# A hybrid decoder layer on one core: fillers kept back behind forgetting-attention stacks, fillers of stick-breaking heads shared out by scan length, and stacks filled by one copy and one subtraction

## The chip, the cores and the metric

The kernel runs on one core of one Trainium2 chip. The metric is device microseconds from the start of the program to its end. Before the change three runs took 2321.92, 2323.00 and 2324.88 us, the median being 2323.0 us.

## What is computed

One decoder layer for 1024 positions of width 1024, in float32. A half step of a SwiGLU network (`x + 0.5 * swiglu(norm(x))`, inner width 2816), then two attentions side by side on the same normed input, a second half SwiGLU step, and a gated embedding. The attentions have eight heads of 64 each:

```
forgetting:      logit[t,s] = q_t.k_s/8 + sum_{s<j<=t} log f_j,  causal softmax, times v
                 (q and k are rms-normed per head, with gains)
stick-breaking:  beta[t,s] = sigmoid(q_t.k_s/8)
                 A[t,s] = beta[t,s] * prod_{s<j<t} (1 - beta[t,j])   for s < t, times v
merged = sigmoid(g_fox) * (y_fox @ w_branch_fox) + sigmoid(g_sb) * (y_sb @ w_branch_sb)
x = x + merged @ w_out
```

Products are made to nearly full float32 precision out of a high part (rounded to the fast matmul type) and a low part (what the rounding lost): high x high + high x low + low x high.

## The kernel before

The program runs stage by stage: first feed-forward step, attention, output projection, second feed-forward step, embedding. The change touches the attention stage, `attention()`, which takes the 16 heads one after the other, 0 to 7 forgetting, 8 to 15 stick-breaking.

**A head.** It has four steps, c = 0 to 3, each with two blocks of 128 queries, i = 2c and 2c + 1. `scores` makes for both blocks the products with all keys up to the block (n = 128(i + 1) columns). It needs the head's *stacks*: Q (128 x 1024, upper 64 partitions the high part of q, lower 64 the low part), KH (the high part of k, twice, on both halves) and KL (the low part of k, twice). The products are the matmuls of lines 1040 (with KH) and 1041 (with KL). Then a forgetting head adds the forget sums and takes row maxima on DVE (line 1045), the exponential on ACT (line 1051), a reciprocal on DVE (line 1052) and the scaling on POOL (line 1053). A stick-breaking head takes two sigmoids on ACT (lines 1048, 1049) and then products along the row by scans on DVE (line 1016), whose time grows with n, and multiplies on POOL (lines 1063 and 1067).

`apply` handles the step before (`prev`), so the scores of step c come between the scores and the values of step c - 1; at c = 0 it is step 3 of the head before. For each pair of key blocks it transposes the probabilities on PE (line 1092, into one of two "pt" banks of PSUM), copies the high part on ACT (line 1094), subtracts on DVE for the low part (line 1095), and multiplies with the values on PE (line 1114). The scans of the step's second block are held in `later` and issued between those subtractions.

**Filling.** Between these pieces the function `take` (called `fill` inside `scores` and `apply`) issues other matmuls, a few at a time: projections for later heads (line 799: v, and q and k of forgetting heads; line 807: q and k of stick-breaking heads, and the gates), and the *forgetting stacks* (line 901: four transposes of normed q and k). These are generators that yield their cost in microseconds after each matmul (0.109 or 0.216). In each head `take` is called 22 times: 7 times at c = 0 (2 in `scores`, 5 in `apply` for the previous head's c = 3), then 4, 5 and 6 times. Each call raises the allowance by total/22, total being the cost of the head's fillers, and issues until the count reaches it; at the head's end `take(True)` drains what is left. PE runs strictly in the order so written (the helper `pe`); the other engines' order comes from the framework's scheduler.

Filling units write to one of two "pf" banks of PSUM. A unit of line 799 or 807 is followed by a copy and mostly a subtraction that empty the bank (lines 105 and 106 for v, 929 for a gate, 965 for the embedding), a stack unit by `fill_stacks`.

**Stacks.** `fill_stacks` gets 512 columns with q on partitions 0 to 63 and k on 64 to 127 in one bank. It makes two copies on ACT (lines 886, 887 with gain for forgetting heads; 881, 882 without for stick-breaking ones), two subtractions on DVE (888, 889 or 883, 884), and two DMAs on the SP queue (890, 891) which bring k's parts to the upper half of KH and KL. Each head needs two such halves; they are made while the head before runs. Stack buffers are two deep. The order in which fillers stand is given by the list `fill`: with forgetting heads a stack half stands between projections, or two halves meet at a head's border (the last of one list and the first of the next, at the starts of heads 2, 4 and 6).

Of the kernel before, what the change touches and what calls it, by code (L numbers as in the profile page):

```python
# [13 lines left out]
AF = mybir.ActivationFunctionType  # L14
ALU = mybir.AluOpType
# [21 lines left out]
def tile_hybrid_decoder_layer(  # L37
# [6 lines left out]
    nc = tc.nc  # L44
# [11 lines left out]
    def slot(tag, shape, dt=F32):  # L56
        pad = -shape[-1] % 16
        t = sb.tile([*shape[:-1], shape[-1] + pad], dt, tag=tag, bufs=BUFS[tag], name=nm(tag))
        return t[:, :, :shape[-1]] if pad else t
# [6 lines left out]
    def bank(tag):  # L66
        return pp.tile([P, 512], F32, tag=tag, bufs=PSUM[tag], name=nm("ps"))

    def ps1():
        ring[0] += 1  # L70
        return bank(("pt", "pf", "pt", "pf")[ring[0] % 4])
# [8 lines left out]
    def pe(ins):  # L80
        order("pe", ins)
# [7 lines left out]
    def f(ap):  # L89
        return ap.bitcast(F32)  # L90
# [783 lines left out]
    def new_stacks():  # L874
        return slot("Q", [P, S], F32R), slot("KH", [P, S], F32R), slot("KL", [P, S], F32R)

    def fill_stacks(stacks, ps, cs, gain=None):
        Q, KH, KL = stacks
        a, b = slice(0, HD), slice(HD, P)
        if gain is None:  # L880
            nc.scalar.copy(Q[a, cs], ps[a, :])
            nc.scalar.copy(KH[b, cs], ps[b, :])
            nc.vector.tensor_sub(Q[b, cs], ps[a, :], f(Q[a, cs]))
            nc.vector.tensor_sub(KL[b, cs], ps[b, :], f(KH[b, cs]))
        else:
            nc.scalar.activation(Q[a, cs], ps[a, :], AF.Copy, scale=gain[a, :])
            nc.scalar.activation(KH[b, cs], ps[b, :], AF.Copy, scale=gain[b, :])
            nc.vector.scalar_tensor_tensor(Q[b, cs], ps[a, :], gain[a, :], f(Q[a, cs]), ALU.mult, ALU.subtract)
            nc.vector.scalar_tensor_tensor(KL[b, cs], ps[b, :], gain[b, :], f(KH[b, cs]), ALU.mult, ALU.subtract)  # L889
        nc.sync.dma_start(f(KH[a, cs]), f(KH[b, cs]))  # L890
        nc.sync.dma_start(f(KL[a, cs]), f(KL[b, cs]))

    def fox_stack_units(cell, hh, out_cell, new_bank=fill_bank):
        def unit(half):
            if half == 0:
                out_cell["st"] = new_stacks()
            cs = slice(half * 512, half * 512 + 512)
            N = cell["n"][half]
            ps = new_bank()
            for q in range(4):  # L900
                pe(nc.tensor.transpose(ps[:, q * P:(q + 1) * P], N[:, q, hh].rearrange("p s d -> p (s d)"), identf[:]))
                yield 0.109
            fill_stacks(out_cell["st"], ps, cs, gqk)
        return [(0.436, unit(0)), (0.436, unit(1))]

    def sb_stack_units(head, out_cell):
        c0 = head * HD

        add_load(out_cell, lambda: wload([kp(win)[:, :, SQ + c0:SQ + c0 + HD], kp(win)[:, :, SK + c0:SK + c0 + HD]], KD, P))

        def unit(half):
            weights(out_cell)
            if half == 0:
                out_cell["st"] = new_stacks()
            ps = bank("pf")
            yield from feat_steps(ps, half, out_cell["w"])
            fill_stacks(out_cell["st"], ps, slice(half * 512, half * 512 + 512))
        return [(24 * 0.216, unit(0)), (24 * 0.216, unit(1))]
# [303 lines left out]
    def attention():  # L1222
# [5 lines left out]
        def fst(h, *to):  # L1228
            return fox_stack_units(qk[h // 2], h % 2, stacks[h], *to)
# [38 lines left out]
        f = [fst(h) for h in range(1, 8)]  # L1268
# [19 lines left out]
        def load_fb(h):  # L1288
            if h < 8:
                head = fox_pairs[h // 2] * 2 + h % 2  # L1290
                fbs[h]["t"] = slot("GF", [P, S])
                nc.sync.dma_start(fbs[h]["t"][:], fd[head].partition_broadcast(P))
# [3 lines left out]
        for h in range(16):  # L1296
            fox = h < 8
            if h % 2 == 0:
                idx = fox_pairs[h // 2] if fox else 4 + (h - 8) // 2
                ys[h // 2] = {"t": slot("Y", [P, S]), "idx": idx}  # L1300
            head = ys[h // 2]["idx"] % 4 * 2 + h % 2
            v = (vf1, vf0, vs0, vs1)[h // 4]
            load_fb(h + 1)
            total = sum(u[0] for u in fill[h])
            state = [0.0, 0.0]
            gens = [u[1] for u in fill[h]]

            def take(last=False):
                state[0] += total / 22
                while gens and (last or state[1] < state[0]):  # L1310
                    cost = next(gens[0], None)
                    if cost is None:
                        gens.pop(0)
                    else:
                        state[1] += cost
            for c in range(4):
                y0, y1 = Y_AT.get((h, c), ((), ()))
                split_y(*y0)
                load_y(*y1)
                step = {"fox": fox, "c": c, "head": head, "st": stacks[h], "v": v, "y": ys[h // 2], "last": h == 15}  # L1320
                if fox:
                    step["fb"] = fbs[h]
                later = []
                scores(step, take, later if prev is not None else None)
                if prev is not None:
                    apply(prev, take, later)
                prev = step
            take(True)
        rest = seq(*[g for _, g in fox_branch[7:]])
        apply(prev, lambda: run(islice(rest, 6)))  # L1330
        run(rest)
        yt = ys[7]["t"]
        for half in range(2):
            cs = slice(half * 512, half * 512 + 512)
# [8 lines left out]
    def load_y(*ks):  # L1343
        for k in ks:
            if k == 0:
                Y_["t"] = slot("X", [P, 4, S])
            nc.sync.dma_start(Y_["t"][:, k % 4, :], yd[k])

    def split_y(*ks):
        for k in ks:  # L1350
            g, i = divmod(k, 4)
            if i == 0:
                yT.append((slot("H", [P, 4, S], F32R), slot("H", [P, 4, S], F32R)))
            hi, lo = yT[g]
            split(hi[:, i, :], lo[:, i, :], Y_["t"][:, i, :], nc.scalar, nc.vector, True)
# [84 lines left out]
    nc.vector.tensor_scalar(gqk[0:HD, :], gqk[0:HD, :], HD ** -0.5, None, ALU.mult)  # L1440

    attention()

    od = dp.tile([4, P, 7, 512], F32, name="branch_sums")
    xm = dp.tile([S, D], F32, name="x_mix")
    for m in range(5, KD):
        w = wload([kp(w_branch_fox[0])[:, :, m * P:(m + 1) * P]], 4, P)
        A.append(slot(("RN", "Q", "KH")[m - 5], [P, S]))
        for half in range(2):
            ps = bank(("sc", "sc", "sc", "pf", "pt", "pf")[2 * (m - 5) + half])  # L1450
# [11 lines left out]
    for m in range(KD):  # L1462
# [13 lines left out]
        for half in range(2):  # L1476
            ps = ps1()
# [161 lines left out]
```

## Time and profile before

| what | us |
|---|---|
| median of three runs | 2323.0 |
| the profiled execution | 2324.2 |
| its span (first to last instruction) | 2322.3 |
| first score matmul of head 0 to that of head 8 | 851.3 to 1144.7 |
| from there to the last value matmul of head 15 | 1144.7 to 1442.7 |

The profiled execution is 1.2 us above the median, and 1.9 us of its time lie outside the span. A row of a group reads: line, engine, operation, tile written <- tiles read, shapes, count | busy us, mean ns of one | idle time of the engine just before them, and what ended it. A row of waits reads: engine, tile and line that waited <- what it waited for: us in total, times, longest. A row of a window reads: stretch, its length, busy time and instructions of PE, PEld (weight loads, beside PE), DVE, ACT and POOL, then the granted TensorE clock, the DMA engines' share and GB/s.

### The profile page before, as it was taken

How to read it: one execution, taken by the hardware profiler on the slowest of the kernel's cores; microseconds unless marked ns; L12 is line 12 of the kernel's file. 1: busy time of each engine (PE TensorE's matmuls, PEld its weight loads, DVE VectorE, ACT ScalarE, POOL GpSimd, SP SyncE). 2: the span in 40 equal slices, each digit the busy share in tenths (PEclk: the TensorE clock that was granted, in tenths of full speed). 3: DMA queues.
4: the chain of work that ended last, by engine and by line, in shares of the span. 5: the costliest groups of instructions: out<-in, count | busy, mean ns of one | idle time of the engine just before them, and what ended most of it. 6: DMA issues, size and time to landing. Idle time of an engine off the chain costs nothing.

```text
span 2322.3 us, 30570 instructions
## 1 busy us (share of the span) xinstructions
PE 2255.0 (97%) x11402; PEld 1909.7 (82%) x11402; DVE 1526.4 (66%) x2296; ACT 1018.1 (44%) x1819; POOL 811.4 (35%) x747
## 2 busy tenths in 40 slices
PE   8999999999999999988998989999999999999999
PEld 6888888888888988988787777888888888888887
DVE  8755555778786336556578787688755555778752
ACT  7333333333454455565655564246333333333431
POOL 2444444200002345645466665500444444200111
PEclk9999999999999999999999999999999999999999
DMA  3333232655233341222202335642333232655232
GB/s 136 108 106 106 98 119 87 228 216 203 92 109 128 110 127 52 60 64 60 64 19 64 87 96 190 220 180 82 106 107 105 100 117 87 227 217 203 74 104 88
DMA packets 179782, 275.48 MB, mean 119 GB/s; under 512 B 26921, under 2 KB 103081, under 8 KB 179634
## 3 DMA queue, kind: packets, MB, share of 16 engines
q1 hardware_dynamic: 179632, 273.53, 35.1%
q8 instruction: 90, 1.47, 0.3%
q14 instruction: 58, 0.48, 0.1%
q10 hardware_dynamic: 2, 0.00, 0.0%
HBM read 189.83 MB, written 75.27 MB: 114 GB/s over the span
## 4 chain that ended last, share of the span: by engine, by line
PE 85%; DVE 8%; ACT 4%; issue 2%; POOL 1%; DMA 0%; SPq 0%; ACTq 0%; DVEq 0%; POOLq 0%
PE ps L556 38%; PE ps L454 21%; PE ps L799 7%; PE ps L1556 4%; DVE RN L1016 3%; PE ps L1361 3%; PE ps L1114 2%; PE ps L807 2%; PE ps L506 2%; PE ps L1092 2%; DVE PT L1095 1%; PE ps L959 1%; PE ps L228 1%; PE ps L1040 1%; PE ps L1041 1%
## 5 line engine op out<-in xcount | busy, mean ns | idle before, releaser
L454 PE MATMUL ps<-H,H 128*128 128x512 f32 x2184 | 497.8, 389 | 1.2 <-DVE X L462 1.2
L454 PEld LDWEIGHTS ps<-H,H 128*128 128x128 f32 x2184 | 409.3, 188 | 86.8 <-issue 2.0
L556 PE MATMUL ps<-H,WL 128*128 128x512 f32 x1116 | 265.0, 389 | 0.8 <-ACT WL L105 0.8
L556 PEld LDWEIGHTS ps<-H,WL 128*128 128x128 f32 x1116 | 209.4, 188 | 44.7 <-ACT WL L105 1.2
L556 PE MATMUL ps<-H,Q 128*128 128x512 f32 x612 | 146.0, 389 | 0.0
L462 DVE SCALAR_TENSOR_TENSOR X<-ps,X 128x512 f32<-128x512 f32 x168 | 108.9, 683 | 51.0 <-PE ps L454 51.0
L1095 DVE TENSOR_TENSOR PT<-ps,PT 128x512 fp32r<-128x512 f32 (+1 forms) x160 | 99.9, 629 | 61.9 <-ACT PT L1094 60.9
L556 PEld LDWEIGHTS ps<-H,Q 128*128 128x128 f32 x612 | 114.9, 188 | 23.9
L799 PE MATMUL ps<-WH,H 128*128 128x256 f32 x768 | 121.7, 296 | 12.2 <-DVE KL L889 7.1
L1114 PE MATMUL ps<-PT,X 128*128 128x256 f32 (+1 forms) x640 | 106.8, 288 | 27.3 <-DVE PT L1095 24.7
L556 PE MATMUL ps<-X,WL 128*128 128x512 f32 x552 | 132.6, 389 | 0.0
L1114 PEld LDWEIGHTS ps<-PT,X 128*128 128x128 f32 x640 | 91.0, 190 | 42.2 <-DVE PT L1095 34.1
L139 POOL TENSOR_TENSOR WL<-RAW,WH 128x512 fp32r<-128x512 f32 (+1 forms) x84 | 99.0, 1201 | 74.6 <-ACT WH L129 42.1
L556 PEld LDWEIGHTS ps<-X,WL 128*128 128x128 f32 x552 | 103.6, 188 | 21.5
L799 PEld LDWEIGHTS ps<-WH,H 128*128 128x128 f32 x768 | 105.5, 197 | 15.3 <-issue 7.7
L1094 ACT CAST PT<-ps 128x512 fp32r<-128x512 f32 (+1 forms) x160 | 87.0, 551 | 65.6 <-PE ps L1092 62.9
L807 PE MATMUL ps<-H,WH 128*128 128x512 f32 x384 | 111.6, 404 | 1.6 <-ACT PT L929 1.6
L219 POOL TENSOR_SCALAR ss<-ss 128x1 f32<-128x1 f32 x28 | 8.5, 304 | 296.9 <-ACT WL L215 231.9
L556 PE MATMUL ps<-H,PT 128*128 128x512 f32 x456 | 108.8, 389 | 0.0
L1053 POOL TENSOR_TENSOR T<-T,l 128x128 f32<-128x128 f32 (+3 forms) x64 | 73.1, 1147 | 98.7 <-DVE l L1052 94.1
L1016 DVE TENSOR_TENSOR_SCAN RN<-GF,RN 128x127 f32<-128x127 f32 (+2 forms) x96 | 102.8, 1071 | 2.6
L1092 PE MATMUL ps<-identf,T 128*128 128x128 f32 x576 | 92.6, 278 | 10.6 <-DVE PT L1095 7.7
(438 smaller groups left out, 4887.2 us busy)
## 6 DMA issues: line engine op xcount, KB each, us to landing
hidden<-PT SPq DMA_DIRECT2D x40, 512.0 KB, 3.1
WH<-in_ffn_w_gate_dram SPq DMA_DIRECT2D x38, 512.0 KB, 5.5
Q<-hidden SPq DMA_DIRECT2D x24, 512.0 KB, 6.8
hidden<-RN SPq DMA_DIRECT2D x22, 512.0 KB, 2.6
KH<-in_ffn_w_up_dram SPq DMA_DIRECT2D x20, 512.0 KB, 6.3
KL<-in_ffn_w_up_dram SPq DMA_DIRECT2D x20, 512.0 KB, 6.9
T<-in_ffn_w_down_dram SPq DMA_DIRECT2D x20, 512.0 KB, 4.4
X<-in_x_dram SPq DMA_DIRECT2D x16, 512.0 KB, 9.5
```

The lines of the kernel that those rows point to most:

```text
L139: ins = eng_lo.tensor_sub(lo[part], raw[part], f(hi[part]))
L454: pe(nc.tensor.matmul(groups[g][t][:], act[:, a, k, t * P:(t + 1) * P], wt[:, b, k, :], start=(fresh and n == 0), stop=(i in (6, 1, 4) and ...
L462: nc.vector.scalar_tensor_tensor(xs, groups[g][t][:], scale, xs, ALU.mult, ALU.add)
L556: pe(nc.tensor.matmul(ps[:], hl[:, a, k, :], rhs(m, b, k), start=(first and i == 0), stop=(final and i == 11), skip_group_check=True))
L799: pe(nc.tensor.matmul(ps[:, :n], hT[t // 4](a, k)[:, (t % 4) * P:(t % 4 + 1) * P], w[k // 4][b][:, k % 4, :n], start=(i == 0), stop=(i == ...
L807: pe(nc.tensor.matmul(ps[:], w[a][:, k, :], hT[half](b, k), start=(i == 0), stop=(i == 23)))
L1016: order("dve", nc.vector.tensor_tensor_scan(*args))
L1092: pe(nc.tensor.transpose(ps[:, col:col + P], step["pr"][j][:, kb * P:(kb + 1) * P], identf[:]))
L1094: high = nc.scalar.copy(pt[:, 0, :width], ps[:, :width])
L1095: low = nc.vector.tensor_sub(pt[:, 1, :width], ps[:, :width], f(pt[:, 0, :width]))
L1114: pe(nc.tensor.matmul(o, lh, r, start=(kpair == c and i == 0), stop=(kpair == 0 and i == 3)))
L1556: pe(nc.tensor.matmul(ps, hT[t // 4](a, k)[:, (t % 4) * P:(t % 4 + 1) * P], pl["w"][d, k // 2][b][:, k % 2, cs], start=(i == 0), stop=(i = ...
```

## The change

Three edits.

1. `fill_stacks` copies all 128 partitions at once to KH, and subtracts all 128 at once into KL. KH[0:64] then holds q's high part and KL[0:64] q's low part; two new DMAs on SP bring them to Q, and then the two old ones overwrite KH[0:64] and KL[0:64] with k's parts. So four DMAs a half instead of two, and the last two may only be issued once the first two have read.
2. `fox_stack_units` yields 1.5 more after `fill_stacks` (`pause`) and counts it in the unit's cost: `take` issues no filling until the allowance has caught up. Where a unit is drained (`run_all` ahead of head 0, `take(True)` at a head's end) the pause has no effect.
3. In stick-breaking heads the filling is no longer spread evenly over the 22 calls, but 14%, 19%, 29% and 38% of it go to c = 0, 1, 2 and 3 (before: 32%, 18%, 23% and 27%). In forgetting heads it stays even.

```diff
         if gain is None:
-            nc.scalar.copy(Q[a, cs], ps[a, :])
-            nc.scalar.copy(KH[b, cs], ps[b, :])
-            nc.vector.tensor_sub(Q[b, cs], ps[a, :], f(Q[a, cs]))
-            nc.vector.tensor_sub(KL[b, cs], ps[b, :], f(KH[b, cs]))
+            nc.scalar.copy(KH[:, cs], ps[:])
+            nc.vector.tensor_sub(KL[:, cs], ps[:], f(KH[:, cs]))
         else:
-            nc.scalar.activation(Q[a, cs], ps[a, :], AF.Copy, scale=gain[a, :])
-            nc.scalar.activation(KH[b, cs], ps[b, :], AF.Copy, scale=gain[b, :])
-            nc.vector.scalar_tensor_tensor(Q[b, cs], ps[a, :], gain[a, :], f(Q[a, cs]), ALU.mult, ALU.subtract)
-            nc.vector.scalar_tensor_tensor(KL[b, cs], ps[b, :], gain[b, :], f(KH[b, cs]), ALU.mult, ALU.subtract)
-        nc.sync.dma_start(f(KH[a, cs]), f(KH[b, cs]))
-        nc.sync.dma_start(f(KL[a, cs]), f(KL[b, cs]))
-
-    def fox_stack_units(cell, hh, out_cell, new_bank=fill_bank):
+            nc.scalar.activation(KH[:, cs], ps[:], AF.Copy, scale=gain[:])
+            nc.vector.scalar_tensor_tensor(KL[:, cs], ps[:], gain[:], f(KH[:, cs]), ALU.mult, ALU.subtract)
+        for dst, src in ((Q[a, cs], KH[a, cs]), (Q[b, cs], KL[a, cs]), (KH[a, cs], KH[b, cs]), (KL[a, cs], KL[b, cs])):
+            nc.sync.dma_start(f(dst), f(src))
+
+    def fox_stack_units(cell, hh, out_cell, new_bank=fill_bank, pause=1.5):
         def unit(half):
...
             fill_stacks(out_cell["st"], ps, cs, gqk)
-        return [(0.436, unit(0)), (0.436, unit(1))]
+            yield pause
+        return [(0.436 + pause, unit(0)), (0.436 + pause, unit(1))]
...
-            state = [0.0, 0.0]
+            state = [0.0, 0.0, 0]
+            share = (7 / 22, 4 / 22, 5 / 22, 6 / 22) if fox else (0.14, 0.19, 0.29, 0.38)
...
             def take(last=False):
-                state[0] += total / 22
+                state[0] += total * share[state[2]] / (7, 4, 5, 6)[state[2]]
...
+                state[2] = c
                 scores(step, take, later if prev is not None else None)
```

What moves on PE at the border of heads 3 and 4, where two stack halves follow each other. Before (line 901 are stack transposes, 1114 values of head 3, 1040 and 1041 scores of head 4, 799 and 807 filling, 1092 probability transposes):

```order
L807 MATMUL ps_8290<-H_4868,WL_7712 128x512 x3
L901 MATMUL ps_8366<-identf,RN_7716 128x128 x4
L1114 MATMUL ps_8313<-PT_8344,X_5815 128x256 x4
L1040 MATMUL ps_8390<-KH_8277,Q_8276 128x128
L1041 MATMUL ps_8390<-KL_8278,Q_8276 128x128
L901 MATMUL ps_8400<-identf,RN_7715 128x128 x4
L799 MATMUL ps_8429<-WH_8178,H_4504 128x256 x3
L1040 MATMUL ps_8437<-KH_8277,Q_8276 128x256
L1041 MATMUL ps_8437<-KL_8278,Q_8276 128x256
L799 MATMUL ps_8429<-WH_8178,H_4504 128x256
```

After, at the same place (lines stand three to four numbers lower: 897 for 901, 1111 for 1114, 1037 and 1038 for 1040 and 1041, 1089 for 1092):

```order
L807 MATMUL ps_8290<-H_4868,WL_7720 128x512 x2
L897 MATMUL ps_8358<-identf,RN_7724 128x128 x4
L1111 MATMUL ps_8317<-PT_8322,X_5815 128x256
L1111 MATMUL ps_8317<-PT_8322,X_5815 128x128 x2
L1111 MATMUL ps_8317<-PT_8322,X_5815 128x256
L1111 MATMUL ps_8317<-PT_8336,X_5815 128x256 x4
L1111 MATMUL ps_8317<-PT_8350,X_5815 128x256 x4
L1037 MATMUL ps_8390<-KH_8251,Q_8250 128x128
L1038 MATMUL ps_8390<-KL_8252,Q_8250 128x128
L897 MATMUL ps_8400<-identf,RN_7723 128x128 x4
L1037 MATMUL ps_8415<-KH_8251,Q_8250 128x256
L1038 MATMUL ps_8415<-KL_8252,Q_8250 128x256
```

The first stack half now stands ahead of all twelve value matmuls, and behind the second one the scores and then the probability transposes (line 1089) follow with no line 799 between.

On PE at c = 0 of head 12, a stick-breaking head; before:

```order
L1040 MATMUL ps_11619<-KH_11273,Q_11272 128x128
L1041 MATMUL ps_11619<-KL_11274,Q_11272 128x128
L807 MATMUL ps_11627<-H_4869,WH_11267 128x512 x4
L1040 MATMUL ps_11635<-KH_11273,Q_11272 128x256
L1041 MATMUL ps_11635<-KL_11274,Q_11272 128x256
L807 MATMUL ps_11627<-H_4868,WH_11267 128x512 x3
L1092 MATMUL ps_11645<-identf,T_11517 128x128
L1092 MATMUL ps_11645<-identf,T_11539 128x128 x2
```

and after:

```order
L1037 MATMUL ps_11619<-KH_11273,Q_11272 128x128
L1038 MATMUL ps_11619<-KL_11274,Q_11272 128x128
L807 MATMUL ps_11627<-H_4869,WH_11267 128x512 x2
L1037 MATMUL ps_11633<-KH_11273,Q_11272 128x256
L1038 MATMUL ps_11633<-KL_11274,Q_11272 128x256
L807 MATMUL ps_11627<-H_4869,WH_11267 128x512
L1089 MATMUL ps_11641<-identf,T_11494 128x128
L1089 MATMUL ps_11641<-identf,T_11533 128x128 x2
```

One or two filling matmuls stand at each call for three or four; over the head's four steps they are 11, 13, 21 and 27 now and were 24, 13, 17 and 20.

On SP, the stack of head 12 (KH_11273, KL_11274, Q_11272) and its neighbours (line 119 loads weights); after:

```order
L887 DMA Q_11272<-KH_11273 64x512
L887 DMA Q_11272<-KL_11274 64x512
L887 DMA KH_11273<-KH_11273 64x512
L887 DMA KL_11274<-KL_11274 64x512
L119 DMA RAW_12240<-in_w_in_dram 128x8x64
L887 DMA Q_11272<-KH_11273 64x512
L887 DMA Q_11272<-KL_11274 64x512
L119 DMA RAW_12240<-in_w_in_dram 128x8x64
L887 DMA KH_11273<-KH_11273 64x512
L887 DMA KL_11274<-KL_11274 64x512
```

There were one KH and one KL row for each half before; a weight load stood between the two of the second half, as one now stands between its two pairs.

## Prediction

> **What bounds the kernel now.** I read the page first, then busy time over the two attention stages, then who TensorE waited for in each, then the instructions around the longest waits. The page's head:
>
> ```profile
> span 2322.3 us, 30570 instructions
> PE 2255.0 (97%) x11402; PEld 1909.7 (82%) x11402; DVE 1526.4 (66%) x2296; ACT 1018.1 (44%) x1819; POOL 811.4 (35%) x747
> ```
>
> PE is busy 97% of the span, so only PE's idle time and its slow clock can be won, and the change touches only the attention. Busy time there, forgetting heads in the first row, stick-breaking heads in the second (length; PE, PEld, DVE, ACT, POOL busy; granted clock; DMA):
>
> ```profile
> 851.30:1144.70 293.40, 267.65 (x1930) 250.24 (x1929) 173.00 (x550) 168.80 (x356) 159.21 (x163) 0.98 0.22 60
> 1144.70:1442.70 298.00, 270.29 (x1572) 231.02 (x1571) 238.75 (x332) 174.37 (x376) 179.71 (x200) 0.98 0.30 87
> ```
>
> PE is idle 25.7 us in the first and 27.7 us in the second, 53 us in all: no more than that, and the slow clock, is in reach. PE's waits, the forgetting stage's six rows ahead, the stick-breaking stage's behind "..." (us in total, times, longest):
>
> ```profile
> PE ps L799 <- DVE KL L889: 7.1, 3, 2.8
> PE ps L799 <- DVE X L106: 4.5, 4, 1.8
> PE ps L807 <- ACT PT L929: 1.6, 1, 1.6
> PE ps L901 <- ACT PT L929: 0.9, 1, 0.9
> PE ps L799 <- ACT PT L965: 0.6, 1, 0.6
> ...
> PE ps L1114 <- DVE PT L1095: 23.2, 24, 1.8
> ```
>
> The five rows of the forgetting stage add up to 14.7 us; all but 0.4 us (one wait at L106) is the first matmul of a filling unit behind a stack's four transposes (L901), or such transposes themselves: 14.3 us. The unit before held one of the two "pf" banks, the stack takes the other for 0.4 us, and then the next unit asks for a bank that nobody has emptied yet. The longest kind, at the start of head 2:
>
> ```profile
> 916.18 0.68 ACT L886 ACTIVATE Q<-ps,gqk 64x512 fp32r<-64x512 f32 x1
> 916.63 0.66 PE L901 MATMUL ps<-identf,RN 128*128 128x128 f32 x4
> 916.87 0.68 ACT L887 ACTIVATE KH<-ps,gqk 64x512 fp32r<-64x512 f32 x1
> 917.59 0.74 DVE L888 SCALAR_TENSOR_TENSOR Q<-ps,gqk,Q 64x512 fp32r<-64x512 f32 x1 [0.36 <-ACT KH L887]
> 918.35 0.76 DVE L889 SCALAR_TENSOR_TENSOR KL<-ps,gqk,KH 64x512 fp32r<-64x512 f32 x1
> 919.25 0.71 PE L799 MATMUL ps<-WH,H 128*128 128x256 f32 x4 [1.97 <-DVE KL L889]
> ```
>
> Two stacks in a row fill both banks; four instructions of some 0.7 us empty the first. Such waits also cost clock. Pairs of rows, a stretch of 3.4 us and the stretch that follows it:
>
> ```profile
> 916.75:920.16 3.41, 1.44 (x12) 1.23 (x12) 2.76 (x7) 2.91 (x7) 0.43 (x2) 1.00 0.17 38
> 920.20:923.60 3.40, 3.40 (x19) 3.40 (x18) 2.24 (x7) 0.99 (x3) 0.03 (x1) 0.50 0.50 116
> 998.70:1002.10 3.40, 0.84 (x7) 0.46 (x5) 1.22 (x4) 3.31 (x6) 1.74 (x2) 1.00 0.14 12
> 1002.10:1008.90 6.80, 5.64 (x27) 5.67 (x27) 4.03 (x11) 3.70 (x8) 1.01 (x2) 0.50 0.66 188
> 1073.80:1077.20 3.40, 1.57 (x13) 1.60 (x14) 2.93 (x5) 1.99 (x5) 0.40 (x1) 1.00 0.23 53
> 1077.20:1080.60 3.40, 3.40 (x18) 3.40 (x17) 1.61 (x7) 1.31 (x4) 0.61 (x1) 0.50 0.44 101
> 1166.00:1169.30 3.30, 1.50 (x10) 1.27 (x9) 3.27 (x4) 0.58 (x2) 3.30 (x3) 1.00 0.00 0
> 1169.40:1172.70 3.30, 3.30 (x14) 2.91 (x13) 3.18 (x6) 2.44 (x6) 2.16 (x4) 0.50 0.99 225
> 1387.80:1391.20 3.40, 1.50 (x8) 1.03 (x7) 3.40 (x4) 1.85 (x3) 1.31 (x2) 1.00 0.93 337
> 1391.20:1398.00 6.80, 6.21 (x20) 5.24 (x21) 6.18 (x7) 2.33 (x8) 5.55 (x6) 0.50 0.45 146
> ```
>
> Each time PE was busy 0.84 to 1.57 us of 3.4, the granted clock in the next stretch was 0.50. The three in the forgetting stage follow the bank waits at the starts of heads 2, 4 and 6; they last 3.4, 6.8 and 3.4 us, and half speed costs half of 13.6: 6.8 us. The two in the other stage last 10.1 us and cost 5.1.
>
> In the stick-breaking stage the waits come in a fixed place. Head 12, its four steps c = 0 to 3:
>
> ```profile
> 1288.50:1297.80 9.30, 9.30 (x60) 8.15 (x59) 4.18 (x8) 4.66 (x10) 2.05 (x5) 1.00 0.07 26
> 1297.80:1302.80 5.00, 4.89 (x27) 4.04 (x26) 4.18 (x5) 3.23 (x7) 4.01 (x4) 1.00 0.76 222
> 1302.80:1310.60 7.80, 7.10 (x41) 5.99 (x41) 7.62 (x12) 5.45 (x13) 7.05 (x9) 1.00 0.82 276
> 1310.60:1322.50 11.90, 9.52 (x53) 7.55 (x52) 11.61 (x14) 7.76 (x15) 7.69 (x8) 1.00 0.06 14
> ```
>
> At c = 0 PE has no gap and DVE is idle more than half; at c = 3 DVE is busy 11.61 of 11.90 us (long scans) and PE idle 2.4 us. That imbalance is what shares by scan length act on.
>
> **The change part by part.** What a stack half's instructions cost (busy us, mean ns, idle before):
>
> ```profile
> L887 ACT ACTIVATE KH<-ps,gqk 64x512 fp32r<-64x512 f32 x16 | 10.9, 682 | 0.3
> L881 ACT CAST Q<-ps 64x512 fp32r<-64x512 f32 x16 | 9.3, 584 | 14.2 <-PE ps L807 14.2
> L889 DVE SCALAR_TENSOR_TENSOR KL<-ps,gqk,KH 64x512 fp32r<-64x512 f32 x16 | 12.1, 757 | 0.4
> L884 DVE TENSOR_TENSOR KL<-ps,KH 64x512 fp32r<-64x512 f32 x16 | 11.1, 695 | 0.4
> L1094 ACT CAST PT<-ps 128x512 fp32r<-128x512 f32 (+1 forms) x160 | 87.0, 551 | 65.6 <-PE ps L1092 62.9 <-ACT T L1051 1.1 <-ACT RN L864 0.6
> L1095 DVE TENSOR_TENSOR PT<-ps,PT 128x512 fp32r<-128x512 f32 (+1 forms) x160 | 99.9, 629 | 61.9 <-ACT PT L1094 60.9 <-DMA RAW<-in_w_in_dram 0.2
> ```
>
> *One copy, one subtraction.* The trace has no 128-partition form of these, but L1094 and L1095 do the like on 128 partitions in 551 and 629 ns (some with 384 columns): no dearer than on 64. So 16 + 16 copies go from ACT (10.9 + 9.3 = 20 us) and as many subtractions from DVE (12.1 + 11.1 = 23 us). Nearly all of it lies beside busy PE; it counts only as a bank that comes free some 1.4 us earlier, and as 0.69 us less DVE at c = 3, both inside the next two terms.
>
> *The two added DMAs a half.* They take the copies' place in Q, and the two old ones now have to wait for the new ones to have read KH and KL. The like of them:
>
> ```profile
> KH<-KH SPq DMA_DIRECT2D x30, 128.0 KB, 2.2
> ```
>
> A stack half is thus ready about two landings behind its subtraction, 4.4 us, not one. I cost it at nothing: columns 512 to 1023 are first read at c = 2, some 12 us later, and the first half of most stacks is ready one step or more ahead. Between nothing and 3 us each for heads 10, 11 and 15 is the bound (rival c).
>
> *Pauses.* Behind fourteen stack halves (those of heads 1 to 7) filling now stays away for 1.5 us of its count. In the new order one or two of the attention's own groups stand between a stack's transposes and the next filling matmul (before, the filling followed at once), so the bank has been emptied by then and the 14.3 us go. What is late next: the attention's own chain, bare of filling there. From transposes to a probability tile's low part there is 0.27 + 0.55 + 0.63 us and two handovers, about 1.6 us, or 2.5 with one stack copy and one subtraction in the queue ahead. Counting in the new order the PE work between the last transposes and the matmuls that need them at the eleven places (at head 5, c = 1, only two stack transposes), the shortfall is 2.5 us against 1.6 and 9.4 against 2.5. The first transposes of the next head may wait for its softmax: 0 to 3.6. Together 2.5 to 13; I take 9, since these queues do hold stack work there. Half clock: two of the three stretches go with their cause, 5.1 of 6.8 us (bounds 0 and 6.8). Forgetting stage: -14.3 + 9 - 5.1 = **-10.4**.
>
> *Shares.* By the order, head 12 gets at c = 0, 1, 2, 3 now 11, 13, 21, 27 filling matmuls for 24, 13, 17, 20 (two fewer here, drained elsewhere). One costs 0.216 us by the count in the kernel; the chain of waits has, for seven in a row,
>
> ```profile
> 1157.27 1.62 PE ps L807 x7
> ```
>
> that is 0.23 each. At c = 0 2.8 us of PE work goes, leaving 6.5. There four rounds of transposes, copy and subtraction over two "pt" banks are serial in pairs; that chain from the step's start I make 7.0 to 8.5 us; I take 7.7: -1.6. At c = 2 0.9 us comes and 0.7 was idle, but not all usable: +0.4. At c = 3 1.5 us comes into 2.4 idle, while DVE loses 0.69 of a step it fills: 0. That is -1.2 a head, eight heads -9.6; bounds -2.6 (c = 0 without a gap) and +1.9 (c = 0 as long as before, and the added work on top of the old waits). One of the two half-clock stretches, that at 1166 in a step that gets more filling, goes: -1.7 (0 to -5.1). Stage: **-11.3**.
>
> Sum: 2324.2 - 10.4 - 11.3 = 2302.5 for the profiled execution. That one was 1.2 us above the median of the runs, so 2301.3: **2301 us**.
>
> *The clock rule.* The rows above give half clock after 3.4 us with PE busy 25 to 46%. [...]
>
> **The rivals.**
> (a) Slower: filling is cover, and where it is taken away the copy-and-subtract chain stands bare. Fourteen pauses then cost the 13 us bound, the half clock stays, and c = 0 stays 9.3 us while c = 2 and 3 grow: -1.3 + 8 x 1.9 = +14, 2337. It decides from +0.7 us a head on, where it eats the 5.3 us that the pauses bring at my price. For it: DVE at 97% of c = 3. Against: DVE is 45% busy at c = 0.
> (b) Shares bring nothing, since DVE sets the head: only the -10.4 stays, 2312.6.
> (c) Stacks come late. DMA queue issues wait behind weight loads:
>
> ```profile
> SPq L119 <- ACT WH L129: 113.7, 18, 25.0
> ```
>
> One such load stood 25 us. If one stands between a stack's DMAs, or landing takes 4 to 5 us, heads 10, 11 and 15 start 1 to 5 us late: about +8, 2309.
> (d) The pauses don't do what they say: the drain at a head's end ignores them, so bank waits stay; then only -11.3, 2312.
> [...]
> (f) Better: new waits 2.5, all half clock of the first stage gone, -2.0 a head: -18.6 - 16 - 1.7 = -36, 2287.
>
> **How the numbers follow.** Forecast 0.42 (own range 2294 to 2308), (a) 0.10, (b) 0.15, (c) 0.08, (d) 0.07, (e) 0.05, (f) 0.13. A range of 2286 to 2318 takes in all but (a) and the far ends of (b) and (f). A measurement tells about 0.2% (4.6 us) from no change. Faster by more 0.81: all but (a), and a part of (b), (c) and (d); within 0.09; slower 0.10.
>
> **What would show it.** In PE's waits the rows of L799 and L807 on the stack's subtraction, L106 and L929 should nearly vanish, and rows of L1114 and L1092 on DVE's L1095 grow in the forgetting stage by 5 to 13 us. Granted clock at the starts of heads 2, 4 and 6 should be 1.00. Head 12 should last 32 to 33 us, c = 0 near 7.7 with small gaps, c = 3 still near 12 with under 1.5 idle. DVE's busy time in the two stages should fall by 23 us and ACT's by 20. A wait of L1040 or L1041 on a DMA of a stack at heads 10, 11 or 15 would be (c). I am wrong if c = 0 stays above 9, or c = 3 grows.

## The result and the profile after

The changed kernel takes **2287.4 us** (median of 4 runs, 2287.38 to 2287.47) against 2323.9 of the kernel before (2321.92 to 2326.29): a ratio of 0.984, 95% interval 0.9825 to 0.986, so 36.5 us less. The forecast was 2301, with a range of 2286 to 2318. The sign was right and the time lies within the range, at its lower end, where rival (f) stood. The gain is 1.7 times the one forecast.

The page's head after the change:

```profile
span 2285.6 us, 30594 instructions
PE 2242.3 (98%) x11402; PEld 1900.6 (83%) x11402; DVE 1498.9 (66%) x2264; ACT 999.5 (44%) x1787; POOL 805.7 (35%) x747
```

Span less PE's busy time is PE's idle time: 67.3 us before, 43.3 now. PE's busy time fell as well, by 12.7 us, with the same 11402 matmuls. Before, the granted clock stood at half for 23.9 us (five stretches), and matmuls took longer there: those of L799 on WH 415 ns between 920.2 and 923.6 us (median of 12) for a median of 283 over the whole trace. Now no stretch of half clock is left between the start and the last microseconds of the program (from 2283.4 us on). DVE lost 27.5 us and ACT 18.6.

The two attention stages, in the columns of before (length; PE, PEld, DVE, ACT, POOL busy; granted clock; DMA):

```profile
851.90:1123.53 271.63, 259.82 (x1931) 244.51 (x1930) 158.84 (x535) 157.73 (x341) 159.41 (x163) 1.00 0.30 82
1123.53:1406.20 282.67, 265.04 (x1572) 227.19 (x1571) 227.89 (x317) 167.71 (x360) 171.74 (x200) 1.00 0.38 105
```

The forgetting stage is 21.8 us shorter (forecast 10.4), the other 15.3 (forecast 11.3). PE's idle time in them is 11.8 us for 25.7, and 17.6 for 27.7. PE's waits after, the forgetting stage ahead of "...", the stick-breaking stage behind:

```profile
PE ps L1089 <- DVE PT L1092: 3.4, 4, 1.1
PE ps L1111 <- DVE PT L1092: 2.8, 5, 1.3
PE ps L1111 <- ACT PT L1091: 2.6, 3, 1.5
PE ps L1089 <- POOL T L1050: 1.3, 1, 1.3
PE ps L799 <- ACT PT L962: 0.3, 1, 0.3
PE ps L799 <- DVE KL L885: 0.2, 1, 0.2
...
PE ps L1111 <- DVE PT L1092: 9.0, 13, 1.0
PE ps L1089 <- DVE PT L1092: 6.5, 7, 1.8
```

The bank waits behind stacks (lines 799, 807 and 897) came to 14.7 us and are 0.7 with a wait of 0.2 at line 897. What is left are waits of the attention's own chain: 10.1 us in the first stage. Those were there before too, and this is the comparison that the prediction did not make: its list of that stage's waits has the five rows of the banks and leaves these four out. The same rows of before, same stage:

```profile
PE ps L1092 <- DVE PT L1095: 5.3, 6, 1.4
PE ps L1114 <- DVE PT L1095: 1.6, 2, 1.2
PE ps L1114 <- ACT PT L1094: 1.5, 1, 1.5
PE ps L1092 <- POOL T L1053: 1.2, 2, 0.8
```

They add up to 9.6. So chain waits grew by 0.5 us, net, under the three edits together, where 9 were forecast.

The start of head 2 after the change, PE alone, the place of the 1.97 us wait that the prediction shows:

```profile
914.81 0.62 PE L897 MATMUL ps<-identf,RN 128*128 128x128 f32 x4
...
915.51 0.28 PE L799 MATMUL ps<-WH,H 128*128 128x256 f32 x1
915.62 0.49 PE L1089 MATMUL ps<-identf,T 128*128 128x128 f32 x3
915.87 1.32 PE L799 MATMUL ps<-WH,H 128*128 128x256 f32 x9
917.03 0.60 PE L1089 MATMUL ps<-identf,T 128*128 128x128 f32 x4
```

None of these rows has a wait in brackets: the scores follow the stack's transposes (L897), then filling (L799) and probability transposes (L1089) alternate. Head 12's steps c = 0, 2 and 3, whose rows of before the prediction has:

```profile
1259.57:1266.46 6.89, 6.82 (x48) 5.95 (x47) 4.18 (x8) 3.61 (x9) 2.15 (x5) 1.00 0.10 38
...
1271.60:1280.57 8.97, 8.30 (x45) 6.76 (x45) 8.79 (x12) 4.39 (x11) 8.38 (x9) 1.00 0.71 222
1280.57:1292.52 11.95, 11.09 (x60) 9.08 (x59) 10.92 (x13) 7.75 (x15) 6.36 (x8) 1.00 0.20 45
```

32.95 us for 34.0. c = 0 went from 9.30 to 6.89 and PE has still hardly a gap there; c = 2 grew from 7.80 to 8.97; c = 3 took 1.6 us more PE work in nearly the same time, 11.95 us for 11.90.

### The profile page after: what moved, and what is told of

Read it like the earlier page. It is cut to its first block, busy times and chain, and to the rows that moved or that the text cites. A ratio compares the mean times of both kernels' runs of the same rounds, so it can differ in the third digit from the quotient of the medians.

```text
span 2285.6 us, 30594 instructions
## 1 busy us (share of the span) xinstructions
PE 2242.3 (98%) x11402; PEld 1900.6 (83%) x11402; DVE 1498.9 (66%) x2264; ACT 999.5 (44%) x1787; POOL 805.7 (35%) x747
## 3 DMA queue, kind: packets, MB, share of 16 engines
q8 instruction: 90, 1.47, 0.3%
## 4 chain that ended last, share of the span: by engine, by line
PE 87%; DVE 7%; ACT 3%; issue 1%; POOL 1%; DMA 1%; SPq 0%; DVEq 0%; ACTq 0%; POOLq 0%
PE ps L556 39%; PE ps L454 21%; PE ps L799 7%; PE ps L1555 4%; PE ps L1360 3%; PE ps L807 3%; DVE RN L1013 3%; PE ps L1111 2%; PE ps L506 2%; PE ps L1089 2%; DVE PT L1092 1%; PE ps L1037 1%; PE ps L1038 1%; PE ps L956 1%; PE ps L228 1%
## 5 line engine op out<-in xcount | busy, mean ns | idle before, releaser
L556 PEld LDWEIGHTS ps<-H,Q 128*128 128x128 f32 x612 | 114.9, 188 | 23.9
L1092 DVE TENSOR_TENSOR PT<-ps,PT 128x512 fp32r<-128x512 f32 (+1 forms) x160 | 99.9, 630 | 49.6 <-ACT PT L1091 48.8
L139 POOL TENSOR_TENSOR WL<-RAW,WH 128x512 fp32r<-128x512 f32 (+1 forms) x84 | 98.1, 1191 | 67.8 <-ACT WH L129 44.5
L1111 PE MATMUL ps<-PT,X 128*128 128x256 f32 (+1 forms) x640 | 103.0, 286 | 15.3 <-DVE PT L1092 11.9
L799 PE MATMUL ps<-WH,H 128*128 128x256 f32 x768 | 115.6, 287 | 0.6 <-ACT PT L962 0.3
L799 PEld LDWEIGHTS ps<-WH,H 128*128 128x128 f32 x768 | 101.4, 190 | 2.1 <-ACT PT L962 0.5
L1089 PE MATMUL ps<-identf,T 128*128 128x128 f32 x576 | 90.6, 275 | 11.6 <-DVE PT L1092 9.9
```

The source lines that it names most:

```text
L139: ins = eng_lo.tensor_sub(lo[part], raw[part], f(hi[part]))
L556: pe(nc.tensor.matmul(ps[:], hl[:, a, k, :], rhs(m, b, k), start=(first and i == 0), stop=(final and i == 11), skip_group_check=True))
L799: pe(nc.tensor.matmul(ps[:, :n], hT[t // 4](a, k)[:, (t % 4) * P:(t % 4 + 1) * P], w[k // 4][b][:, k % 4, :n], start=(i == 0), stop=(i == ...
L1089: pe(nc.tensor.transpose(ps[:, col:col + P], step["pr"][j][:, kb * P:(kb + 1) * P], identf[:]))
L1092: low = nc.vector.tensor_sub(pt[:, 1, :width], ps[:, :width], f(pt[:, 0, :width]))
L1111: pe(nc.tensor.matmul(o, lh, r, start=(kpair == c and i == 0), stop=(kpair == 0 and i == 3)))
```

## The experiments

All times are medians beside runs of the kernel before in the same job (2324.8 to 2325.7 us); the differences are to those, a ratio of 0.9900 being 23 us.

**One edit at a time.** Three kernels, each the one before with one edit: `stacks_only` edit 1, `pause_only` edit 2, `shares_only` edit 3. The diffs are the hunks shown under "The change".

> The kernel before with the one copy, one subtraction and four DMAs a stack half alone; no pause, even shares. Theory A (the gain is PE time: bank waits, the half clock that follows them, and filling where DVE is slow): a bank comes free some 1.4 us earlier, which shortens the three waits of L799 on a stack's subtraction (7.1 us) to about 3, and 0.7 us of DVE a stick-breaking head at c = 3: 4 to 10 us faster, 2313 to 2320, with waits of filling on L106 and L929 behind stacks still there (6 to 7 us). Theory B (the gain is the 43 us of ACT and DVE work taken away): more than half of the 36.5 us comes from this edit, 2305 or less.

> The kernel before with the pause of 1.5 alone. Theory A: the bank waits behind stacks (14.3 us) go, the three half-clock stretches of the forgetting stage (6.8 us) go with them, little comes back in waits of L1114 and L1092: 15 to 21 us faster, 2303 to 2309, granted clock 1.00 at the starts of heads 2, 4 and 6. Theory B: half of it or less, 2313 or more, since the stack's two copies and two subtractions still hold the queues ahead of the probabilities.

> The kernel before with the shares by scan length alone. Theory A: c = 0 of a stick-breaking head falls from 9.3 to about 7, c = 2 and 3 grow by half a us or less each: 9 to 14 us faster, 2310 to 2315; the forgetting stage is as before. Theory B: without the lighter stacks DVE at c = 3 is still full, and the added filling adds to its waits: 5 us faster or less, 2319 or more.

Measured: stacks_only **2303.4, -21.8** (ratio 0.9914, 0.9899 to 0.9929); pause_only **2316.4, -8.8** (0.9966, 0.9955 to 0.9978); shares_only **2316.8, -8.4** (0.997, 0.9959 to 0.9982). The sum, -39, is close to the -36.5 of all three. The edit that the prediction gave nothing of its own brings more than the other two together. What edit 1 does, in the waits of the forgetting stage of stacks_only:

```profile
PE ps L799 <- DVE X L106: 4.7, 4, 1.8
PE ps L1088 <- DVE PT L1091: 3.9, 5, 1.1
PE ps L799 <- DVE KL L885: 2.2, 3, 1.3
PE ps L807 <- ACT PT L925: 1.6, 1, 1.6
PE ps L1110 <- ACT PT L1090: 1.5, 1, 1.5
PE ps L1088 <- POOL T L1049: 1.5, 1, 1.5
```

With a wait of 0.6 more at L799 and one of 0.4 at the stack's own transposes the bank waits are 9.5 us (14.7 before). Half clock lasts 6.8 us in its trace for 23.9: the stretches at the starts of heads 2, 4 and 6 are gone.

What the pauses do without edit 1, the forgetting stage of pause_only:

```profile
PE ps L1093 <- DVE PT L1096: 6.7, 7, 1.7
PE ps L1115 <- ACT PT L1095: 5.1, 4, 1.7
PE ps L1115 <- DVE PT L1096: 3.6, 6, 1.4
PE ps L799 <- DVE KL L889: 2.2, 3, 1.7
```

Bank waits are down to 2.5 us (2.2 and one of 0.3), and the chain waits, with 0.9 for POOL, up to 16.3 from 9.6: +6.7, half of what the pauses save in bank waits. That comes near the prediction's 9, but here a stack puts two copies and two subtractions into the queues of ACT and DVE. With the light stack it is less: the same rows come to 7.2 us in no_pause (below) and to 10.1 in the kernel after, +2.9.

**Half clock tested by itself.** Stack transposes at the starts of heads 2, 4 and 6 are issued six times over, so that PE is busy in place of its longest waits (60 matmuls more, nothing else changed):

```diff
-            for q in range(4):
-                pe(nc.tensor.transpose(...))
-                yield 0.109
+            for again in range(6 if half == 0 and border else 1):
+                for q in range(4):
+                    pe(nc.tensor.transpose(...))
+                    if not again:
+                        yield 0.109
```

> The kernel before, in which the four stack transposes at the starts of heads 2, 4 and 6 are issued six times over into the same bank (twenty more transposes each, 2.2 us of PE work, 6.6 us in all), where PE waits 7.1 us for banks. No result changes. If the half clock hangs on PE's idle time in the stretch before, the three stretches at half clock go: 5 to 8 us faster, 2316 to 2319. If the half clock comes from something else (what the PE array does in the heads' starts, or its weights), the work only takes the place of the wait: 2322 to 2325 with the clock at 0.50 as before.

Measured: **2320.3, -4.9** (0.998, 0.9971 to 0.999), between the two. 60 matmuls more, and the kernel is faster. The same places as in the prediction's pairs of rows, head 2 and head 4:

```profile
916.00:919.40 3.40, 3.40 (x33) 3.40 (x32) 2.31 (x6) 2.40 (x6) 1.00 (x1) 1.00 0.16 36
1000.00:1003.40 3.40, 2.80 (x25) 2.60 (x24) 2.17 (x6) 3.32 (x6) 0.40 (x1) 1.00 0.94 223
```

PE is busy, and no stretch of half clock follows at any of the three borders. So at these three borders the half clock hung on PE's idle time in the stretch before it: it followed on 1.44, 0.84 and 1.57 us of PE work in before, and not on the 3.40 and 2.80 us of these rows; the granted clock of the whole stage is 1.00 for 0.98. The balance of the two traces: half clock went from 23.9 to 10.2 us, which is worth 6.8, and idle time fell by 5.0, while PE's work grew by 7.8; the span is 4.1 us shorter. The second stage's stretch at 1169 went as well, and one came up at 1209.6, where before had none.

**Bank or queue?** Edit 1 frees the bank some 1.4 us earlier (at the start of head 2 a stack's first copy and last subtraction span 2.93 us in before, 916.18 to 919.11, and 1.47 in stacks_only, 913.75 to 915.22) and takes work from two queues. To part these, the work is put back where it can't hold the bank: edit 1, and behind each copy and subtraction one more of 64 partitions that only touches SBUF (its result goes nowhere). `dummy_dve` has the subtraction alone.

```diff
             nc.scalar.copy(KH[:, cs], ps[:])
+            nc.scalar.copy(spare[a, :], f(KH[a, cs]))
             nc.vector.tensor_sub(KL[:, cs], ps[:], f(KH[:, cs]))
+            nc.vector.tensor_sub(spare[b, :], f(KH[b, cs]), f(KH[b, cs]))
```

(and the same with gain for the forgetting heads).

> The kernel before with edit 1 alone (one copy, one subtraction, four DMAs), and behind each copy and each subtraction of a stack half one more of 64 partitions that reads and writes SBUF only (its result is not used). So the filling bank comes free as early as with edit 1, but ACT and DVE have about as many instructions as before. Edit 1 alone gave 2303.4, -21.8. Theory K (the early bank brings it): most stays, 2303 to 2309. Theory Q (the queues bring it: the attention's own copies and subtractions stood behind 32 + 32 stack instructions of 0.6 to 0.75 us): most is lost, 2315 to 2325. In between: both, in the share that the time shows.

> The kernel before with edit 1 alone, and behind each subtraction of a stack half one more of 64 partitions on VectorE that touches SBUF only (its result is not used); ScalarE keeps its single copy. Edit 1 alone gave 2303.4, with work put back on both engines it was 2315.9: 12.5 us lie between. If VectorE's queue is what edit 1 relieved (VectorE is busy 11.6 of 11.9 us at c = 3): 2312 to 2317. If ScalarE's (its copies stand ahead of VectorE's subtractions in each chain): 2303 to 2307. If both: 2308 to 2312.

Measured: stacks_dummy **2315.9, -8.9** (0.9963, 0.995 to 0.9976); dummy_dve **2318.5, -6.4** (0.9971, 0.9959 to 0.9984). More than half of edit 1's gain goes when the work comes back, and DVE's subtraction alone takes at least as much back: what edit 1 relieved beside the bank is VectorE's queue, and ScalarE's 20 us brought nothing that shows. A part of that comes by way of the clock: from the trace of stacks_only to that of dummy_dve the span grows by 14.3 us, of which 7.6 are PE's idle time and 6.8 half clock (6.8 us of it became 20.5). The forgetting stage's waits in stacks_dummy:

```profile
PE ps L1094 <- DVE PT L1097: 5.0, 6, 1.5
PE ps L799 <- DVE X L106: 4.5, 4, 1.8
PE ps L799 <- DVE KL L890: 2.3, 3, 1.4
PE ps L1116 <- DVE PT L1097: 1.7, 2, 1.4
PE ps L807 <- ACT PT L931: 1.6, 1, 1.6
PE ps L1116 <- ACT PT L1096: 1.5, 1, 1.5
```

This parts the two. Bank waits, with one more of 0.6: 9.0 us, as low as with edit 1; the early bank made that. Chain waits, with 1.3 for POOL: 9.5, the 9.6 of before again, where edit 1 had 7.2 (3.9 + 1.5 + 1.5, and one of 0.3 at L1110). Half clock is back to 17.1 us from 6.8, PE's idle time over the span to 62.8 from 56.4. One reservation on the size: the subtraction put back is dearer than the one removed (DVE, dummy_dve):

```profile
L889 DVE SCALAR_TENSOR_TENSOR spare<-KH,gqk 64x512 f32<-64x512 f32 x16 | 15.0, 939 | 0.5
L885 DVE TENSOR_TENSOR spare<-KH 64x512 f32<-64x512 f32 x16 | 14.7, 919 | 0.5
```

29.7 us are put back for 23 removed, so the queue's part, 12.9 to 15.4 of 21.8 us, is an upper bound. The traces show where the extra comes from. Of the 16 rows of L889, the eight with no POOL instruction beside them took 744 to 752 ns, as the removed ones did (744 and 757 on average), and five with POOL busy beside them for more than half of their time took 751 to 2007. The removed ones read PSUM and took 743 to 758 ns with POOL busy or not. So the work put back was slower beside POOL as well; in the forgetting stage PE's waits for POOL are 3.1 us in dummy_dve and 1.5 in stacks_only.

**Which heads?** `stacks_fox` is the kernel before with edit 1 only in the branch with gain, that of the forgetting heads.

> The kernel before with edit 1 in the stacks of the forgetting heads alone (16 halves); those of the stick-breaking heads keep two copies and two subtractions. In the trace of edit 1 alone TensorE's idle time fell by 8.5 us in the forgetting stage and 1.4 in the other, and its time at half clock by 16.9 us (8.4 us of work). If the gain is local to the stage and the half clock of the first stage hangs on its bank waits: -8.5 and -6.8, so 2309 +- 2. If the queues of the stick-breaking stage bring as much, half of 21.8: 2314. If the half clock falls by chance of its phase, anything from 2307 to 2317 with the clock in the second stage to match.

Measured: **2309.9, -14.9** (0.9939, 0.9924 to 0.9954), the local reading. Idle time fell by 9.7 us in the forgetting stage (278.34 us long, PE busy 262.25) and rose by 0.9 in the other; half clock is 13.7 us for 23.9. The remaining 7 us are left to the stick-breaking stacks, by difference.

**One edit left out.** `no_pause` has edits 1 and 3, `no_stacks` has 2 and 3.

> Edits 1 and 3 without the pauses. If the edits add up as they did alone (-21.8, -8.4, with -8.8 for the pauses): 2294 to 2296, so the pauses are worth 6 to 9 us on top. If edit 1 makes the pauses needless, because the bank is free 1.4 us earlier: 2287 to 2290. If the pauses carry the stage, as the prediction had it, the bank waits of 14.3 us return in part (9 of them were left with edit 1 alone): 2298 to 2302.

> Edits 2 and 3 without edit 1 (two copies and two subtractions stay). The prediction gave edit 1 nothing of its own, which would make this 2287 to 2292. If the edits add up as they did alone (-8.8, -8.4): 2306 to 2308. If pauses and shares hurt each other without the lighter stacks (more filling at c = 3, where DVE is full, and bare chains): 2310 to 2318.

Measured: no_pause **2295.6, -29.2** (0.9876, 0.986 to 0.9893); no_stacks **2309.1, -15.7** (0.9937, 0.9922 to 0.9951). Both lie within 1.5 us of what the single edits add up to (-30.2 and -17.2). On top of the other two the pauses are worth 8 us (2295.6 to 2287.4) and edit 1 22 (2309.1 to 2287.4). The idle time shows what is additive: in the forgetting stage the pauses take 5.4 us from it without edit 1 (25.7 to 20.4) and 5.4 with it (17.2 to 11.8). In the stick-breaking stage the shares take 5.1 us without edit 1 (27.7 to 22.6) and 8.9 with it (26.3 to 17.4). Without it the wait moves; the stick-breaking stage of shares_only:

```profile
PE ps L1092 <- DVE PT L1095: 11.9, 11, 2.7
PE ps L1114 <- DVE PT L1095: 7.1, 11, 1.0
```

The wait of the value matmuls falls from 23.2 to 7.1, and the wait of the transposes (L1092) rises from 2.4 to 11.9. Of these, 6.9 us fall at c = 0, where before had none: there the chain now has less filling to cover it. With the light stack the row is 6.5, 3.7 of it at c = 0.

**Better than the change?** The kernel after with other numbers: `pause_09` pauses of 0.9 for 1.5; `shares_more` shares of 0.09, 0.19, 0.29, 0.43; `shares_10_13` these shares for heads 10 to 13 alone.

```diff
-            share = (7 / 22, 4 / 22, 5 / 22, 6 / 22) if fox else (0.14, 0.19, 0.29, 0.38)
+            share = (7 / 22, 4 / 22, 5 / 22, 6 / 22) if fox else (0.09, 0.19, 0.29, 0.43)
```

> The kernel after with pauses of 0.9 of the count in place of 1.5. Without pauses it is 2295.6, with 1.5 it is 2287.4; in the trace without pauses the first filling matmul waits 0.4 to 1.8 us behind a stack, mostly 1.2 to 1.6, and with 1.5 the attention's own chain waits about 1 us at heads 1 and 4. If the bank's being empty is all that counts: 2289 to 2293, as a part of the pauses is now too short. If 1.5 is too long since edit 1 empties the bank sooner: 2284 to 2287.

> The kernel after with shares of 0.09, 0.19, 0.29, 0.43 for the stick-breaking heads: some four filling matmuls, 0.9 us, move from c = 0 to c = 3. In the kernel after c = 0 lasts 6.9 us in five of the eight heads with TensorE busy all of it, and c = 3 lasts 12.0 to 14.0 with TensorE idle 0.9 to 2.4. If the chain at c = 0 has its floor at 7 to 8.5 us, as the prediction had it, nothing goes at c = 0 and the time is 2287 to 2291. If the floor is lower and c = 3 takes the work into its idle time: up to 0.7 us a head, 2282 to 2285. If VectorE's full c = 3 grows by what comes, or the bare c = 0 brings half clock back: 2289 to 2296.

> The kernel after with the shares 0.09, 0.19, 0.29, 0.43 for heads 10 to 13 alone. With these shares for all eight heads, heads 10 to 13 became 0.4, 1.2, 0.6 and 0.9 us shorter, heads 14 and 15 each 1.1 longer, and three stretches of half clock came back, two of them in the forgetting stage, which the shares don't touch. If the heads are independent: idle time falls by 3 us, 2284 to 2285. If the half clock comes back with it: 2286 to 2289, and runs that differ by 1 to 3 us, where the kernel after's four agreed within 0.1 us.

Measured: pause_09 **2289.2** (0.9844, 0.9829 to 0.9859), shares_more **2287.4** (0.9837, 0.9822 to 0.9851), shares_10_13 **2286.4** (0.9834, 0.982 to 0.9848). None can be told from the change itself (0.9843, 0.9825 to 0.986). Head 11's c = 0 and c = 3, of after and of shares_more:

```profile
1226.64:1233.56 6.92, 6.86 (x49) 5.95 (x47) 4.66 (x9) 3.60 (x9) 4.83 (x7) 1.00 0.58 143
1246.01:1259.57 13.56, 11.30 (x60) 9.02 (x59) 11.86 (x12) 6.82 (x14) 9.53 (x9) 1.00 0.35 79
```

```profile
1228.16:1234.95 6.79, 6.24 (x44) 5.22 (x43) 4.67 (x9) 3.81 (x10) 4.72 (x7) 1.00 0.58 145
1247.62:1259.94 12.32, 11.79 (x64) 9.67 (x62) 10.08 (x12) 7.26 (x15) 9.63 (x8) 1.00 0.14 29
```

c = 0 got 0.6 us less PE work and is only 0.1 shorter: now there is a gap, and this is near its floor (6.6 to 6.9 us at heads 11 to 14 in shares_more and shares_10_13). c = 3 got more filling and is shorter; DVE is busy 1.8 us less there, in as many instructions (12). Two scans account for 1.6 of it: the first, of 128 columns, took 1.20 us in after, where POOL was subtracting weights (L139) from 1247.81 to 1250.47, and 0.43 in shares_more, where POOL had nothing to do until 1250.29; the next, of 383 columns, took 1.86 and 1.04. That this shift of POOL's work would repeat with other shares is not shown. Idle time in the stage falls by 2.2 us, but heads 14 and 15 lose 1.1 each, and 10.2 us of half clock came back. In pause_09 one wait costs the gain:

```profile
PE ps L799 <- DVE X L106: 3.3, 1, 3.3
```

PE is idle 3.3 us at a bank of head 1 that the v unit has not emptied, and 6.8 us of half clock follow.

## Where the prediction was right, and where it failed

| term | forecast | shown by the traces |
|---|---|---|
| forgetting: bank waits behind stacks | -14.3 | -14.0 (14.7 to 0.7) |
| forgetting: new chain waits | +9 | +0.5 (9.6 to 10.1) |
| forgetting: half clock | -5.1 | -6.8 |
| stick-breaking: the shares | -9.6 | -10.1 (idle 27.7 to 17.6) |
| stick-breaking: half clock | -1.7 | -5.1 |

*Bank waits*: right, in size and place. The pauses and edit 1 share them: the pauses alone leave 2.5 us, edit 1 alone 9.5.

*New chain waits*: here the prediction failed. "Together 2.5 to 13; I take 9, since these queues do hold stack work there." Its count had one stack copy and one subtraction in the queue, that is the light stack, and there the pauses added 2.9 us (no_pause to after), near the lower bound; 6.7 is what they added with the heavy one (pause_only). The two edits act on one queue, and the sum left out what edit 1 takes from the waits that stood there, 2.4 us (9.6 to 7.2): net +0.5. The sentence in which it went wrong is the earlier one, that edit 1 "counts only as a bank that comes free some 1.4 us earlier, and as 0.69 us less DVE at c = 3, both inside the next two terms": stacks_dummy has that early bank and brings 8.9 of 21.8 us. The rest, as an upper bound, came out of VectorE's queue, in which the low part of a probability tile no longer stands behind two stack subtractions. "Nearly all of it lies beside busy PE" was true of the 23 us as a sum and false of the moments that count, when PE waits for that queue. So the bound of 2.5 was wrong as a net figure too: it counted only what the pauses could add.

*Half clock, 11.9 us where 6.8 were forecast*: that it follows on waits was right, the size wrong. The prediction tied single stretches to single waits. What the traces show is a count over all stretches of 3.4 us (last section): with PE busy under 1.52 us all 18 were followed by half clock, above 1.87 none of 2254. A wait that goes can lift a stretch over these figures, and after has none below 1.88. A stretch of 3.4 us and the one behind it, of pause_09 and of after:

```profile
894.00:897.40 3.40, 0.73 (x5) 0.39 (x3) 0.14 (x2) 0.67 (x1) 3.40 (x5) 1.00 0.01 2
897.40:904.20 6.80, 6.13 (x27) 6.13 (x28) 3.96 (x17) 2.25 (x6) 2.86 (x5) 0.50 0.64 155
```

```profile
1102.40:1105.80 3.40, 1.86 (x10) 1.25 (x9) 0.85 (x5) 3.17 (x7) 2.66 (x5) 1.00 0.44 102
1105.90:1109.30 3.40, 3.25 (x19) 2.83 (x19) 2.31 (x9) 0.66 (x2) 0.73 (x1) 1.00 0.50 124
```

This is the stretch of after with the least PE work, and the clock stays at 1.00. That the half clock would not hang on these waits, (e) in the prediction's chances with 0.05, is out: busy_border removes only the waits at three borders, and their three stretches go (23.9 us of half clock before, 10.2 there).

*Shares*: the sum was right, the parts were not. The mean step over the eight heads (from the first score matmul to the next step's) went by -2.6, 0, -0.1 and +0.75 us at c = 0 to 3, where -1.6, 0, +0.4 and 0 were forecast; the half clock's 0.6 a head is in it. c = 3 grew in seven of the eight heads, which the prediction had named as a sign that it was wrong; what c = 0 gave beyond the forecast made up for it, so that the sum came out was luck in part. The floor of c = 0 was put at 7.0 to 8.5 us and is 6.6 to 6.9.

*New DMAs at no cost*: right. No wait of any size for a stack's DMA stands in the forgetting or the stick-breaking rows of after, so rival (c) did not happen; nor did (a), (b) or (d). The like of it, one wait of 0.3 us by a score matmul of the forgetting stage, is in stacks_only, stacks_fox and no_pause. Rival (f), 2287, came closest, in its terms as well: new waits (net) below 2.5, no half clock in the forgetting stage, -2.0 us a head. In the two stages DVE's busy time fell by 25.0 us and ACT's by 17.7, for 23 and 20.

The books close. If time is PE's work, its idle time and half of the time at half clock, then span less the other two must be the same in every kernel with the same matmuls:

| kernel | span | PE idle | half clock | PE busy less half of it |
|---|---|---|---|---|
| before | 2322.3 | 67.3 | 23.9 | 2243.0 |
| after | 2285.6 | 43.3 | 0 | 2242.3 |
| stacks_only | 2301.8 | 56.4 | 6.8 | 2242.0 |
| pause_only | 2311.7 | 62.3 | 10.2 | 2244.3 |
| shares_only | 2314.7 | 61.4 | 20.5 | 2243.1 |
| stacks_dummy | 2313.9 | 62.8 | 17.1 | 2242.6 |
| dummy_dve | 2316.1 | 64.0 | 20.5 | 2241.9 |
| no_pause | 2293.6 | 47.9 | 6.8 | 2242.3 |

The last column is flat within 2.4 us. (Left out is the half clock of each trace's last microseconds.) Of the 36.7 us of span, 24.0 are idle time and 11.9 clock.

What stays open: why ScalarE's relief shows no gain while its copies stand in the same chains (dummy_dve is 2.6 us slower than stacks_dummy, the intervals overlap), and how much of the half clock in a single trace is owed to the edit and how much to where the stretches happen to fall.

## What to carry to other kernels

Price an edit that takes instructions off an engine by the moments when the bottleneck waits for that engine's queue, not by the engine's idle share; taking away 64 instructions of some 0.7 us, on engines at 44% and 66%, was worth 21.8 us here, 8.9 of it with as much work as before in the queues. When two edits act on one queue, price the second one with the first in place, and set new waits against the old ones of the same kind in the trace of before. Price a wait of TensorE here at more than itself where it empties a stretch: all 18 stretches of 3.41 us with under 1.52 us of PE work were followed by 3.4 or 6.8 us at half clock, 25 of 44 with 1.52 to 1.87 us, none of 2254 with more. By an estimate from the table above, whose last column is flat within 2.4 us, half of the time at half clock is lost.

## What the hardware showed that was not expected

The half clock came in units of 3.4 us (3.4 or 6.8 in the attention of each trace that has it; 3.413 and 6.827 in before's clock record, where the first and last stretch in the attention, at 920.158 and 1391.197 us, begin 138 units of 3.413 apart). Laid on each trace as a grid of 3.413 us, in step with its stretches of half clock, the attention of the fourteen traces, from the first score matmul to the last value matmul, gives 2316 stretches at full clock. Of those with PE busy under 1.52 us all 18 were followed by half clock, of 44 with 1.52 to 1.87 us 25, of 2254 above that none (in before and after alone 3 of 3, 2 of 5 and none of 320). Six stretches at half clock were followed by another one; in them PE was busy up to 2.95 us, by estimate 1.5 us of work at the full clock (half of 2.95, at a granted clock of 0.50). The highest that was followed by half clock, in no_stacks, and one that was not, in before:

```profile
897.40:900.80 3.40, 1.82 (x12) 1.67 (x13) 2.56 (x10) 1.30 (x4) 3.14 (x6) 1.00 0.18 42
900.80:904.20 3.40, 3.40 (x17) 3.40 (x16) 2.66 (x13) 1.30 (x3) 0.82 (x2) 0.51 0.00 0
```

```profile
1049.90:1053.30 3.40, 1.59 (x14) 1.35 (x13) 1.73 (x8) 2.81 (x8) 3.40 (x3) 1.00 1.01 204
1053.30:1056.70 3.40, 2.74 (x19) 2.42 (x20) 2.79 (x6) 0.85 (x2) 3.32 (x3) 1.00 0.68 151
```

The lowest stretch of after, 1102.40 to 1105.81, has 1.88 us on this grid, just above the highest that was followed by half clock (1.86). shares_10_13 has the forgetting stage of after unchanged, and yet a stretch of half clock in it. Its grid lies 0.6 us later there, and the stretch ahead of the half clock, 1102.98 to 1106.39, has 1.73 us of PE work. The twelve kernels of the experiments, which all have half clock in the attention, vary by 1.1 to 4.7 us over their 4 to 10 runs; the four runs of after agree within 0.09 us.

The stacks' copies and subtractions of 512 columns took about the same on 128 partitions (after) as on 64 (before): 688 and 748 ns with gain for 682 and 757, 600 and 673 without for 584 and 695. The subtraction that reads PSUM took the same with POOL busy beside it or not: 743 to 746 ns in all 16 rows of before's L888, 8 of them beside POOL, and 756 to 758 in all 16 of L889, 5 of them beside POOL. The one that reads SBUF alone did not: 744 to 752 ns alone, up to 2007 beside POOL (dummy_dve, 64x512). Nor did the scans, which read SBUF alone: over the fourteen traces 112 scans of 128 columns with no POOL instruction beside them took 406 to 418 ns, 85 with POOL's weight subtraction (L139) beside them for over half of their time 444 to 1485, with a median of 828.
